# The first block's shift and scale from TensorE in quarters of the channels, and the ahead-of-time weight splits through another pool and VectorE

## The chip, the cores and the metric

The kernel runs on one core of a Trainium2 chip. The metric is the time of one execution of the whole program on the device in microseconds (us), here the median of several runs. TensorE's clock has two levels, 1.2 and 2.4 GHz; the profile gives the share of it that was granted.

## The reference, cut to what matters

Two layers work on 512 tokens of 1024 channels, 256 context tokens and 256 latent tokens. Each layer has a feed-forward block, a mixer of four token mixers, and a second feed-forward block. Every block first normalises its input and then shifts and scales it per channel; shift, scale and gate come from a vector of the stream (context or latent) through one large matrix per layer:

```
mod   = (silu(c)     @ ada_w[l] + ada_b[l]).reshape(1, 1, 3, 3, D)     # latent tokens
mod_c = (silu(c_ctx) @ ada_w[l] + ada_b[l]).reshape(1, 1, 3, 3, D)     # context tokens

def ffn_step(s, m, j, f):
    hm = layer_norm(s) * (1 + m[:, :, j, 1]) + m[:, :, j, 0]           # modulate: scale, shift
    y = swiglu(hm, ffn_w_in[f], ffn_w_out[f])
    return post_norm(s, 0.5 * m[:, :, j, 2] * y, j)                    # m[j, 2]: gate
```

`ada_w[l]` is 1024 x 9216 in 32-bit floats: 9 groups (3 blocks, and shift, scale and gate in each) of 1024 columns. The two groups that the change is about, shift and scale of block 0 of layer 0, are 8 MB of it. `w_in[l]`, the input matrix of the mixer, is cut into 70 chunks of 128 columns.

## The kernel before, in words

All matrix products of the big weights are done with three matmuls in place of one: each operand is split into a rounded high part (ScalarE casts, L123, L159) and the rest as the low part (a subtraction on GpSimd or VectorE, L124, L161), and high x high, high x low and low x high are summed in PSUM (`mm3`, L413 to L415). Weights come as pairs of raw chunks; the list `self.lo` says chunk by chunk whether GpSimd (P) or VectorE (D) subtracts.

`first` (L318) is the start of the program. It loads the tokens, takes the mean and variance on VectorE (L348 to L351), and normalises on ScalarE (L355). Then it goes over the eight channel groups k of 128 channels. For each k it needs shift and scale of 128 channels and two streams: four dot products over 1024 values, each one VectorE instruction (L374) over a transposed 128 x 1024 piece of `ada_w` and a copy of silu(c) on all partitions (`cb`), with a sum at its end. For k above 3 one of the four is a product on GpSimd (L370) and a sum on ScalarE (L371). `cb` is made by a matmul with a column of ones (L340) and Silu on ScalarE (L341). After the dots, two small VectorE instructions add the bias (L381) and 1 (L382); four transposes of the normalised tokens (L385) land in PSUM, ScalarE shifts and scales them in two halves (L390), and `split` (L159, L161) gives the two parts of `H[k]`.

What follows is the first feed-forward block (`ffn`, with `start` set to the two weight pairs that `first` loaded): for each k, 12 matmuls of 512 columns go into four PSUM banks, 96 matmuls in all; I call these the start block. After it come the other weight chunks in order. Between them, at points written in the code (`fill.pop(0)()`), lie fillers: the dot products for all other shifts, scales and gates (`ada_dot`, L199 loads and L203 multiplies), and in two of the four feed-forward blocks `presplit`.

`presplit` (L127) takes one chunk of layer 1's `w_in` in two halves of 512 columns: it loads the half on SyncE's queue (L136), ScalarE casts the high part (L138) and writes it to DRAM (L139, ScalarE's queue), GpSimd subtracts (L140) and writes the low part to DRAM (L141, GpSimd's queue). The mixer of layer 1 then only loads both parts. 38 chunks are done so: 14 in the second feed-forward block of layer 0 and 24 in the first of layer 1, 76 halves in all. Its three tiles come from the pool T (six tiles of 128 x 512). Pool C (two tiles) serves the post-norm at the end of a feed-forward block and the convolution in the mixer.

Other pools: F (five), Y (four) and B (two) hold tiles of 128 x 2048; PSUM has three banks for pm, three for pg and two for px. The instruction order of each engine is not written by hand: a planner goes through the program in order of priority with estimated durations, hands out the tiles, and fixes for every engine and every queue one order. On the chip each queue goes through its order and waits where it has to.

Of the kernel before, what the change touches and what calls it, by code (L numbers as in the profile page):

```python
# [52 lines left out]
class Net:  # L53
# [73 lines left out]
    def presplit(self, l, i):  # L127
        nc = self.nc
        dst = self.dr.tile([P, 2048], F32, name=f"pre{l}_{i}")
        self.pre[l, i] = dst  # L130

        def go():
            for k in range(2):
                c = slice(k * 512, (k + 1) * 512)
                raw = self.T()
                nc.sync.dma_start(raw, self.t["win"][l, i][:, c])  # L136
                h, lo = self.T(F32R), self.T(F32R)
                nc.scalar.copy(h, raw)  # L138
                nc.scalar.dma_start(dst[:, c], h.bitcast(F32))  # L139
                nc.gpsimd.tensor_sub(lo, raw, h.bitcast(F32))  # L140
                nc.gpsimd.dma_start(dst[:, 1024 + k * 512:1024 + (k + 1) * 512], lo.bitcast(F32))  # L141

        return go
# [14 lines left out]
    def split(self, hi, lo, src, pool_lo=True):  # L158
        self.nc.scalar.copy(hi, src)  # L159
        eng = self.nc.gpsimd if pool_lo else self.nc.vector  # L160
        eng.tensor_sub(lo, src, hi.bitcast(F32))  # L161
# [156 lines left out]
    def first(self):  # L318
        nc = self.nc
        V = nc.vector  # L320
        row = self.slot("B", name="row")[:1]
        nc.sync.dma_start(row, self.t["cc"].rearrange("s d -> (s d)").unsqueeze(0))
        ones = self.small(P, "vn")
        V.memset(ones, 1.0)
        self.x = [self.Y(name="x") for _ in range(2)]
        wa = []

        def load_ada():
            k = len(wa)
            wa.append(self.slot("FY"[k % 2], name="wa").rearrange("p (a c) -> p a c", a=2))  # L330
            nc.sync.dma_start(wa[k], self.t["adaw"][0, k:k + KD + 1:KD].rearrange("a p c -> p a c"))

# [3 lines left out]
        load_ada()  # L336
        self.cb = self.sb.tile([P, 2, D], F32, tag="B", bufs=2, name="cb")
        for e in range(4):
            ps = self.ps()
            nc.tensor.matmul(ps, ones[:1], row[:, e * 512:(e + 1) * 512], start=True, stop=True)  # L340
            nc.scalar.activation(self.cb[:, e // 2, (e % 2) * 512:(e % 2 + 1) * 512], ps, AF.Silu)  # L341
        xn = []
        for s in range(2):
# [7 lines left out]
            last = V.scalar_tensor_tensor(nm, mv[:, 0::2], -1.0, r, op0=ALU.mult, op1=ALU.mult)  # L351
# [4 lines left out]
        H = self.new_h()  # L356
        m, ab = self.modT[0], self.adab[:, 0]
        ws = []
        for k in range(KD):
            pair = slice(k, k + KD + 1, KD)  # L360
            if k and k < KD - 1:
                load_ada()
            w = wa[k]
            with self.tc.issue_after(last.ins) if k == 1 else nullcontext():
                for a in range(2):
                    for s in range(2):
                        acc = m[:, k + KD * a, s:s + 1]
# [8 lines left out]
                if k < 2:  # L376
                    self.lo = "P"
                    ws.append(self.pair(self.t["f1"][0, 0, 2 * k:2 * k + 2], "F", (None, "F" if k else None)))
                    if not k:
                        load_ada()  # L380
            V.tensor_add(m[:, pair], m[:, pair], ab[:, pair].unsqueeze(2).to_broadcast([P, 2, 2]))  # L381
            V.tensor_scalar(m[:, k + KD], m[:, k + KD], 1.0, None, op0=ALU.add)  # L382
            ps = self.ps("pg")
            for t in range(4):
                nc.tensor.transpose(ps[:, t * P:(t + 1) * P], xn[t][k // 4][:, k % 4 * P:(k % 4 + 1) * P], self.ident)  # L385
            hf = self.T()
            for s in range(2):
                c = slice(256 * s, 256 * s + 256)
                sh, sc = m[:, k, s:s + 1], m[:, k + KD, s:s + 1]
                nc.scalar.activation(hf[:, c], ps[:, c], AF.Identity, bias=sh, scale=sc)  # L390
            self.split(H[0][:, k], H[1][:, k], hf, pool_lo=k > 2)
# [1148 lines left out]
def lay(a):  # L1540
# [7 lines left out]
    o["adab"] = c(a["ada_b"].reshape(L, 72, P).transpose(2, 0, 1))  # L1548
    o["norm_g"], o["norm_b"] = c(a["norm_g"]), c(a["norm_b"])
# [51 lines left out]
```

## Time and profile before

| | us |
|---|---|
| median of 3 runs | 2805.08 |
| the runs | 2803.21 to 2805.39 |
| profiled execution | 2813.55 |
| its span in the trace | 2811.8 |
| TensorE busy | 2603.6 (93%) |
| VectorE busy | 1937.6 (69%) |
| ScalarE busy | 1101.7 (39%) |
| GpSimd busy | 1017.2 (36%) |

One execution was profiled. PE is TensorE's matmuls, PEld its weight loads, DVE is VectorE, ACT ScalarE, POOL GpSimd, and SP SyncE, which here only issues DMAs. Matmuls are pipelined, and a "busy" TensorE need not be at its full pace; the count of matmuls in a stretch tells more than the busy time.

### The profile page before, as it was taken

What the parts mean: (1) busy time and instruction counts of PE and PEld (TensorE: products, weight loads), DVE (VectorE), ACT (ScalarE), POOL (GpSimd) and SP (SyncE); (2) the same over time, 40 slices, a digit from 0 to 9 for tenths busy, and PEclk for the clock granted to TensorE, in tenths of its full rate; (3) what the DMA queues carried; (4) which work ended last, traced back from release to release, by engine and by line L of the source; (5) the groups of instructions that cost most, each with busy time, mean ns of one, the idle gap of its engine ahead of it and who ended that gap; (6) DMA issues with size and microseconds to landing.
All of it is one profiled execution on the core that took longest, in us unless ns stands there. A gap on an engine that the chain in (4) does not pass through costs nothing.

```text
span 2811.8 us, 38509 instructions
## 1 busy us (share of the span) xinstructions
PE 2603.6 (93%) x14382; PEld 2182.3 (78%) x14382; DVE 1937.6 (69%) x3150; ACT 1101.7 (39%) x2033; POOL 1017.2 (36%) x784
## 2 busy tenths in 40 slices
PE   5999989998898999999989999999999989888998
PEld 3787878776776787879768888777887977777897
DVE  8695966768899835265887662629568899756455
ACT  3322235483333434354322353332444544344443
POOL 4323223222544344436542336662310056411221
PEclk8999999999999999999999999999999999999899
DMA  5555542234432334437874438875364764357353
GB/s 225 188 180 172 191 156 98 73 109 130 137 108 84 113 124 120 164 105 258 293 258 151 164 113 283 309 260 199 103 229 165 237 184 147 124 158 254 120 189 105
DMA packets 195372, 476.73 MB, mean 170 GB/s; under 512 B 32641, under 2 KB 72801, under 8 KB 194161
## 3 DMA queue, kind: packets, MB, share of 16 engines
q1 hardware_dynamic: 174242, 424.40, 46.0%
q10 hardware_dynamic: 14832, 29.89, 3.0%
q0 software_dynamic: 6112, 19.99, 1.9%
q8 instruction: 113, 1.85, 0.3%
q14 instruction: 73, 0.60, 0.1%
HBM read 400.77 MB, written 73.45 MB: 169 GB/s over the span
## 4 chain that ended last, share of the span: by engine, by line
PE 31%; DVE 10%; DMA 6%; issue 4%; POOL 2%; ACT 2%; SPq 0%; ACTq 0%; POOLq 0%; DVEq 0%
PE pm L414 8%; PE pm L415 8%; PE pm L413 8%; DVE junk L203 3%; DMA T<-in_win_dram 2%; DVE wl L124 2%; DMA wa<-in_adaw_dram 1%; DMA pre<-T 1%; DMA wr<-in_wo_dram 1%; DVE G L898 1%; PE px L415 1%; PE px L414 1%; PE px L413 1%; DVE C L1141 1%; PE pg L907 0%
## 5 line engine op out<-in xcount | busy, mean ns | idle before, releaser
L415 PE MATMUL pm<-h,wl 128*128 128x512 f32 (+1 forms) x2512 | 897.7, 358 | 34.9 <-DVE wl L124 34.2
L413 PE MATMUL pm<-h,wh 128*128 128x512 f32 (+1 forms) x2512 | 900.3, 360 | 29.5 <-ACT h L159 12.1
L414 PE MATMUL pm<-h,wh 128*128 128x512 f32 (+1 forms) x2512 | 896.5, 357 | 12.1 <-DVE h L161 6.3
L415 PEld LDWEIGHTS pm<-h,wl 128*128 128x128 f32 x2512 | 488.1, 194 | 109.2 <-DVE wl L124 41.6
L413 PEld LDWEIGHTS pm<-h,wh 128*128 128x128 f32 x2512 | 487.4, 195 | 101.8 <-ACT h L159 14.6
L123 ACT CAST wh<-wr 128x1024 fp32r<-128x1024 f32 x304 | 318.7, 1049 | 605.9 <-PE pm L414 206.6
L414 PEld LDWEIGHTS pm<-h,wh 128*128 128x128 f32 x2512 | 488.7, 195 | 80.8 <-POOL h L161 9.1
L124 DVE TENSOR_TENSOR wl<-wr,wh 128x1024 fp32r<-128x1024 f32 x196 | 276.3, 1410 | 288.8 <-ACT wh L123 287.4
L124 POOL TENSOR_TENSOR wl<-wr,wh 128x1024 fp32r<-128x1024 f32 x108 | 277.6, 2571 | 418.2 <-ACT wh L123 385.3
L203 DVE SCALAR_TENSOR_TENSOR junk<-wa,cb 128x1024 bf16<-128x1024 f32 x256 | 382.1, 1535 | 2.7 <-DMA wa<-in_adaw_dram 1.8
L161 POOL TENSOR_TENSOR F<-G,F 128x512 fp32r<-128x512 f32 (+1 forms) x94 | 135.2, 1439 | 352.3 <-ACT F L159 328.1
L1141 DVE SCALAR_TENSOR_TENSOR C<-C,vec 128x482 f32<-128x482 f32 (+29 forms) x240 | 176.0, 733 | 4.5 <-ACT C L1133 1.4
L414 PE MATMUL pm<-wl,F 128*128 128x512 f32 x368 | 145.6, 396 | 1.7 <-DVE wl L124 1.3
L413 PE MATMUL pm<-wh,F 128*128 128x512 f32 x368 | 145.5, 396 | 1.6 <-ACT G L425 1.6
L415 PE MATMUL pm<-wh,F 128*128 128x512 f32 x368 | 144.1, 395 | 0.0
L140 POOL TENSOR_TENSOR T<-T 128x512 fp32r<-128x512 f32 x76 | 110.6, 1456 | 81.8 <-ACT T L138 80.5
L427 DVE TENSOR_TENSOR G<-G,pm 128x512 f32<-128x512 f32 (+1 forms) x93 | 54.4, 585 | 121.7 <-PE pm L415 97.4
L902 POOL TENSOR_TENSOR wk<-wk,cd 128x512 f32<-128x512 f32 x56 | 70.4, 1259 | 135.6 <-PE pg L924 88.4
L124 DVE TENSOR_TENSOR wl<-raw,wh 128x1024 fp32r<-128x1024 f32 x61 | 75.0, 1231 | 63.5 <-ACT wh L123 63.5
L159 ACT CAST F<-G 128x512 fp32r<-128x512 f32 (+1 forms) x94 | 50.9, 541 | 160.3 <-DVE G L427 160.3
L606 DVE SCALAR_TENSOR_TENSOR G<-pm,vec,G 128x506 f32<-128x506 f32 (+5 forms) x126 | 87.3, 693 | 23.5 <-ACT G L601 21.8
L123 ACT CAST wh<-raw 128x1024 fp32r<-128x1024 f32 x64 | 66.8, 1047 | 85.8 <-PE pm L414 40.7
(411 smaller groups left out, 4595.0 us busy)
## 6 DMA issues: line engine op xcount, KB each, us to landing
wr<-in_f_dram SPq DMA_DIRECT2D x204, 512.0 KB, 4.1
wa<-in_adaw_dram SPq DMA_DIRECT2D x72, 1024.0 KB, 5.1
wr<-in_win_dram SPq DMA_DIRECT2D x94, 512.0 KB, 3.6
raw<-in_f_dram SPq DMA_DIRECT2D x30, 1024.0 KB, 5.0
T<-in_win_dram SPq DMA_DIRECT2D x76, 256.0 KB, 4.9
pre<-T ACTq DMA_DIRECT2D x76, 256.0 KB, 4.1
pre<-T POOLq DMA_DIRECT2D x76, 256.0 KB, 4.5
wl<-pre SPq DMA_DIRECT2D x36, 512.0 KB, 5.2
```

What stands on the lines that cost most here:

```text
L123: nc.scalar.copy(h, r)
L124: (nc.gpsimd if pool_lo else nc.vector).tensor_sub(l, r, h.bitcast(F32))
L140: nc.gpsimd.tensor_sub(lo, raw, h.bitcast(F32))
L161: eng.tensor_sub(lo, src, hi.bitcast(F32))
L203: nc.vector.scalar_tensor_tensor(junk, w3[:, a], 1.0, self.cb[:, s], op0=ALU.mult, op1=ALU.mult, accum_out=self.modT[l][:, i + a, s:s + 1])
L413: nc.tensor.matmul(ps, wh, xh, start=first, stop=False)
L414: nc.tensor.matmul(ps, wh, xl, start=False, stop=False)
L415: nc.tensor.matmul(ps, wl, xh, start=False, stop=last)
L427: nc.vector.tensor_mul(hf[:, c], sg[:, c], pu[:, c])
L606: nc.vector.scalar_tensor_tensor(acc[:, :, d:], src[:, :, :n - d], w(j), acc[:, :, d:], op0=ALU.mult, op1=ALU.add)
L902: nc.gpsimd.tensor_mul(S(d, n + 1).rearrange("p (h e) -> p h e", h=4), S(d, n).rearrange("p (h e) -> p h e", h=4), gs["cd"][:, d * N_CH + ...
L1141: V.scalar_tensor_tensor(o, x, w(j), o, op0=ALU.mult, op1=ALU.add)
```

## The change

There are two parts.

In `presplit` the loaded half comes from pool C in place of T, and the subtraction is done by VectorE in place of GpSimd. The write of the low part stays on GpSimd's queue.

In `first` the dot products go. The two groups of `ada_w` come in their own layout (1024 rows on the partitions, `ada0`), in four quarters q of 256 channels, shift and scale of a quarter in 1 MB each, into tiles of the pools Y, B and F. silu(c) lies as 32 columns per row group, two of them filled (`ct`). For each quarter 16 matmuls with 32 stationary columns and 256 moving columns run in four column groups of the array (partitions 0, 32, 64 and 96 of one PSUM bank), each group summing two of the eight row groups; VectorE copies the bank to SBUF (a tile of T); four matmuls with a two-column selector `sel` add the four groups and turn the result so that channels lie on partitions; VectorE adds the bias and 1. The transposes of the two channel groups of the quarter stand ahead of these matmuls in the program. Shift and scale of the tokens is now half on ScalarE and half on VectorE, and all splits of `H` subtract on VectorE; two of the four splits of the first weights go to VectorE as well (`self.lo = "PD"`). `cb`, which the later dot products need, is loaded and put through Silu by `load_c` (L176) after the last split.

```
 presplit
-                raw = self.T()
+                raw = self.unit("C")
                 nc.sync.dma_start(raw, self.t["win"][l, i][:, c])
                 ...
-                nc.gpsimd.tensor_sub(lo, raw, h.bitcast(F32))
+                nc.vector.tensor_sub(lo, raw, h.bitcast(F32))
 split
-        self.nc.scalar.copy(hi, src)
+        self.last = self.nc.scalar.copy(hi, src).ins
 first
-        row = self.slot("B", name="row")[:1]
-        nc.sync.dma_start(row, self.t["cc"].rearrange("s d -> (s d)").unsqueeze(0))
-        ones = self.small(P, "vn")
-        V.memset(ones, 1.0)
+        cs = self.T()
+        raw, sel = cs[:, 256:272], cs[:, 272:274]
+        nc.scalar.dma_start(cs[:, 256:274], self.t["ccT"])
...
-        load_ada()
-        self.cb = self.sb.tile([P, 2, D], F32, tag="B", bufs=2, name="cb")
-        for e in range(4):
-            ps = self.ps()
-            nc.tensor.matmul(ps, ones[:1], row[:, e * 512:(e + 1) * 512], start=True, stop=True)
-            nc.scalar.activation(self.cb[:, e // 2, (e % 2) * 512:(e % 2 + 1) * 512], ps, AF.Silu)
+        def load_ada(q):
+            for kind in range(2):
+                w = self.slot(("YB", "FF", "YB", "YB")[q][kind], name="wa")
+                nc.sync.dma_start(w, self.t["ada0"][q, kind])
+                wa[q, kind] = w.rearrange("p (k c) -> p k c", k=KD)
+        def load_w(k):
+            self.lo = "PD"
+            ws.append(self.pair(self.t["f1"][0, 0, 2 * k:2 * k + 2], "F", (None, "F" if k else None)))
+        load_ada(0)
+        load_w(0)
+        load_ada(1)
+        V.memset(cs[:, :256], 0.0)
+        ct = cs[:, :256].rearrange("p (k c) -> p k c", k=KD)
+        nc.scalar.activation(ct[:, :, :2], raw.rearrange("p (k s) -> p k s", k=KD), AF.Silu)
...
-        for k in range(KD):
...
-                        if k > 3 and a and s:
-                            j = self.sb.tile([P, D], F32, tag="R", bufs=2, name="prod")
-                            nc.gpsimd.tensor_mul(j, w[:, a], self.cb[:, s])
-                            nc.scalar.activation(j, j, AF.Identity, accum_out=acc)
-                        else:
-                            j = self.sb.tile([P, D], BF16, tag="M", bufs=2, name="junk")
-                            V.scalar_tensor_tensor(j, w[:, a], 1.0, self.cb[:, s], op0=ALU.mult, op1=ALU.mult,
-                                                   accum_out=acc)
...
+        for q in range(4):
+            if q == 1:
+                load_w(1)
+            if q in (1, 2):
+                load_ada(q + 1)
+            pk = []
+            for k in (2 * q, 2 * q + 1):
+                ps = self.ps("pg")
+                for t in range(4):
+                    nc.tensor.transpose(ps[:, t * P:(t + 1) * P], xn[t][k // 4][:, k % 4 * P:(k % 4 + 1) * P],
+                                        self.ident)
+                pk.append(ps)
+            pa = self.ps("pg")
+            for kind in range(2):
+                o = slice(256 * kind, 256 * kind + 256)
+                for r in range(2):
+                    for i in range(4):
+                        nc.tensor.matmul(pa[32 * i:32 * i + 32, o], ct[:, 4 * r + i], wa[q, kind][:, 4 * r + i],
+                                         start=r == 0, stop=r == 1)
+            sb = self.T()
+            nc.vector.tensor_copy(sb, pa)
+            pt = self.ps("px")[:, :8]
+            for i in range(4):
+                nc.tensor.matmul(pt[:, 2 * i:2 * i + 2], sb[:, i * P:(i + 1) * P], sel, start=True, stop=True)
+            k2 = slice(2 * q, 2 * q + 2)
+            V.tensor_add(m4[:, :, k2], pt.rearrange("p (a k s) -> p a k s", a=2, k=2),
+                         ab4[:, :, k2].unsqueeze(3).to_broadcast([P, 2, 2, 2]))
+            V.tensor_scalar(m4[:, 1, k2], m4[:, 1, k2], 1.0, None, op0=ALU.add)
+            for k, ps in zip((2 * q, 2 * q + 1), pk):
+                hf = self.T()
+                for s in range(2):
+                    c = slice(256 * s, 256 * s + 256)
+                    sh, sc = m[:, k, s:s + 1], m[:, k + KD, s:s + 1]
+                    if s:
+                        V.tensor_scalar(hf[:, c], ps[:, c], sc, sh, op0=ALU.mult, op1=ALU.add)
+                    else:
+                        nc.scalar.activation(hf[:, c], ps[:, c], AF.Identity, bias=sh, scale=sc)
+                self.split(H[0][:, k], H[1][:, k], hf, pool_lo=False)
+        with self.tc.issue_after(self.last):
+            self.load_c()
```

## Rows read from the trace of the kernel before

**Rows 1.** Windows of 40 us: length, busy us and count per engine, PEclk, DMA share, GB/s
```profile
40.00:80.00 40.00, 26.02 (x91) 18.44 (x90) 39.67 (x57) 14.14 (x26) 20.11 (x9) 0.81 0.43 151
...
1400.00:1440.00 40.00, 32.83 (x124) 26.05 (x125) 40.00 (x48) 12.11 (x17) 22.75 (x14) 0.87 0.86 295
1440.00:1480.00 40.00, 35.51 (x148) 28.41 (x148) 26.03 (x30) 11.81 (x15) 14.22 (x10) 0.96 0.64 220
...
1720.00:1760.00 40.00, 40.00 (x176) 32.71 (x175) 17.56 (x15) 14.84 (x20) 27.54 (x26) 1.00 0.86 282
```
**Rows 2.** Groups of VectorE's instructions in the first 84 us, busy us and mean ns
```profile
L374 DVE SCALAR_TENSOR_TENSOR junk<-wa,cb 128x1024 bf16<-128x1024 f32 x28 | 47.1, 1716 | 0.0
```
**Rows 3.** Waits in the first 90 us: total us, times, longest
```profile
ACT T L390 <- DVE modT L382: 32.3, 6, 12.0
```
**Rows 4.** Timeline of TensorE at the start block: start us, us, instruction, idle before
```profile
66.14 0.63 PE L414 MATMUL pm<-h,wh 128*128 128x512 f32 x1
66.57 0.63 PE L415 MATMUL pm<-h,wl 128*128 128x512 f32 x1
...
81.57 0.39 PE L415 MATMUL px<-h,wF 128*128 128x512 f32 x1
...
86.50 0.80 PE L415 MATMUL pm<-h,wl 128*128 128x512 f32 x1 [2.36 <-DVE wl L124]
```
**Rows 5.** Windows of 5 us at the start, columns as in the first group
```profile
0.00:5.00 5.00, 2.13 (x3) 1.12 (x4) 0.22 (x2) 1.34 (x2) 0.93 (x5) 1.00 0.52 170
...
10.00:15.00 5.00, 0.05 (x2) 0.03 (x1) 4.39 (x13) 1.49 (x3) 1.18 (x2) 1.00 1.03 418
```
**Rows 6.** Timeline of ScalarE: the normalised tokens
```profile
14.11 5.75 ACT L355 ACTIVATE G<-x,bnm,br 128x512 f32<-128x512 f32 x8 [3.45 <-DVE bnm L351]
```
**Rows 7.** Timeline of TensorE in layer 0's mixer, small fp32 matmuls (two records each)
```profile
768.03 1.35 PE L1275 MATMUL px<-ident,T 128*128 128x128 f32 x8
769.31 0.64 PE L888 MATMUL pg<-wk,gt 128*32 128x128 f32 x16
769.88 1.10 PE L1281 MATMUL px<-kv,T 128*128 128x64 f32 x8
...
772.83 1.95 PE L907 MATMUL pg<-vn,G 128*128 128x128 f32 x16
```
**Rows 8.** Groups of VectorE's instructions over the whole span
```profile
L911 DVE TENSOR_TENSOR wk<-pg,wk 128x512 f32<-128x512 f32 x56 | 38.2, 684 | 11.3 <-PE pg L907 10.9
...
L427 DVE TENSOR_TENSOR G<-G,pm 128x256 f32<-128x256 f32 x34 | 14.3, 421 | 50.3 <-PE pm L415 40.5 <-POOL F L161 4.0 <-ACT G L425 3.6
```
**Rows 9.** Groups of ScalarE's instructions in the first 84 us
```profile
L390 ACT ACTIVATE T<-pg,modT 128x256 f32<-128x256 f32 x16 | 8.1, 559 | 32.3 <-DVE modT L382 32.3
...
L159 ACT CAST h<-T 128x512 fp32r<-128x512 f32 x8 | 5.0, 619 | 0.3
```
**Rows 10.** Tile cb at its second load, 1200 to 1320 us: ns min/median/max
```profile
L182 ACT ACTIVATE cb<-cb x2: 1062/1062/1062, 1226.6 to 1228.0; 128x1024 f32<-128x1024 f32 x2
...
DMA to landing us min/median/max: 6.4/6.9/7.4
```
**Rows 11.** Timeline of VectorE: first and last step of the first gate, its first use
```profile
71.60 1.21 DVE L203 SCALAR_TENSOR_TENSOR junk<-wa,cb 128x1024 bf16<-128x1024 f32 x1
...
102.90 2.36 DVE L210 TENSOR_TENSOR modT<-modT,adab 128x16 f32<-128x16 f32 x1
...
144.30 1.28 DVE L560 TENSOR_TENSOR M<-pm,gate 128x512 f32<-128x512 f32 x2
```
**Rows 12.** Tile T: subtraction of the presplits; idle of engines before instructions on T
```profile
L140 POOL TENSOR_TENSOR T<-T x76: 1257/1296/2272, 1281.4 to 1886.4; 128x512 fp32r<-128x512 f32 x76
...
  ACT T L138: 81.0, 41
```
**Rows 13.** Timelines of VectorE and GpSimd at one presplit
```profile
1404.25 2.28 DVE L203 SCALAR_TENSOR_TENSOR junk<-wa,cb 128x1024 bf16<-128x1024 f32 x1
...
1403.19 2.27 POOL L140 TENSOR_TENSOR T<-T 128x512 fp32r<-128x512 f32 x1 [4.90 <-ACT T L138]
```

More of the change, by code (lines that the diff above doesn't have):

```diff
@@ L320, in first @@
         V = nc.vector
-        row = self.slot("B", name="row")[:1]
-        nc.sync.dma_start(row, self.t["cc"].rearrange("s d -> (s d)").unsqueeze(0))
-        ones = self.small(P, "vn")
-        V.memset(ones, 1.0)
+        cs = self.T()
+        raw, sel = cs[:, 256:272], cs[:, 272:274]
+        nc.scalar.dma_start(cs[:, 256:274], self.t["ccT"])
         self.x = [self.Y(name="x") for _ in range(2)]
[L326 to L331, printed above, removed]
         for t in range(4):
@@ L335, in first @@
             nc.sync.dma_start(self.x[t // 2][:, o], self.t["xall"][t // 2][:, o])
-        load_ada()
-        self.cb = self.sb.tile([P, 2, D], F32, tag="B", bufs=2, name="cb")
-        for e in range(4):
-            ps = self.ps()
-            nc.tensor.matmul(ps, ones[:1], row[:, e * 512:(e + 1) * 512], start=True, stop=True)
-            nc.scalar.activation(self.cb[:, e // 2, (e % 2) * 512:(e % 2 + 1) * 512], ps, AF.Silu)
+        wa = {}
+        def load_ada(q):
[3 more added lines that the diff above has]
+                wa[q, kind] = w.rearrange("p (k c) -> p k c", k=KD)
+        ws = []
+        def load_w(k):
[7 more added lines that the diff above has]
+        nc.scalar.activation(ct[:, :, :2], raw.rearrange("p (k s) -> p k s", k=KD), AF.Silu)
         xn = []
@@ L350, in first @@
             r, nm = self.rstd(mv[:, 1::2], LN_EPS, 2, "b"), self.small(2, "bnm", 2)
-            last = V.scalar_tensor_tensor(nm, mv[:, 0::2], -1.0, r, op0=ALU.mult, op1=ALU.mult)
+            V.scalar_tensor_tensor(nm, mv[:, 0::2], -1.0, r, op0=ALU.mult, op1=ALU.mult)
             for e in range(2):
@@ L357, in first @@
         m, ab = self.modT[0], self.adab[:, 0]
-        ws = []
-        for k in range(KD):
[L360 to L367, printed above, removed]
-                        if k > 3 and a and s:
-                            j = self.sb.tile([P, D], F32, tag="R", bufs=2, name="prod")
-                            nc.gpsimd.tensor_mul(j, w[:, a], self.cb[:, s])
-                            nc.scalar.activation(j, j, AF.Identity, accum_out=acc)
-                        else:
-                            j = self.sb.tile([P, D], BF16, tag="M", bufs=2, name="junk")
-                            V.scalar_tensor_tensor(j, w[:, a], 1.0, self.cb[:, s], op0=ALU.mult, op1=ALU.mult,
-                                                   accum_out=acc)
[L376 to L391, printed above, removed]
@@ new lines, in first @@
+        m4 = m[:, :2 * KD].rearrange("p (a k) s -> p a k s", a=2)
+        ab4 = ab[:, :2 * KD].rearrange("p (a k) -> p a k", a=2)
+        for q in range(4):
[36 more added lines that the diff above has]
+                self.split(H[0][:, k], H[1][:, k], hf, pool_lo=False)
@@ L1548, in lay @@
     o["adab"] = c(a["ada_b"].reshape(L, 72, P).transpose(2, 0, 1))
+    w = a["ada_w"][0, :, :2 * D].reshape(KD, P, 2, 4, 256)
+    o["ada0"] = c(w.transpose(3, 2, 1, 0, 4).reshape(4, 2, P, 2048))
+    q = np.arange(P)[:, None] % 32 == np.arange(2)[None, :]
+    o["ccT"] = c(np.concatenate([o["cc"].reshape(2, KD, P).transpose(2, 1, 0).reshape(P, 16), q], 1).astype(np.float32))
     o["norm_g"], o["norm_b"] = c(a["norm_g"]), c(a["norm_b"])
```

## Prediction

> **What bounds the kernel now.** I read the windows first, then the waits and timelines of the two places that the change touches. In a good stretch TensorE does 176 matmuls in 40 us, 0.227 us each, the last row of [rows 1]. Against that pace two places stand out.
>
> The first is the start. In 40 to 80 us TensorE does 91 matmuls while VectorE is busy 39.67 of 40 us [rows 1]. What fills VectorE are the 28 dots of shift and scale, 47.1 us [rows 2]; ScalarE's shift and scale waits 32.3 us for their result [rows 3] and TensorE waits behind it. The last matmul of the start block starts at 81.57 us [rows 4]. So the start is bound by VectorE, and a shorter way to shift and scale moves the whole rest of the program.
>
> The second are the stretches with presplits. In 1400 to 1480 us TensorE does 124 + 148 = 272 matmuls in place of 352, so 80 x 0.227 = 18 us are lost, with VectorE full in the first half [rows 1]. In the other presplit stretch, in layer 1, VectorE is busy 17.56 of 40 us and TensorE loses nothing (the last of [rows 1]).
>
> **Part one, the start.** Three floors for the end of the start block:
>
> - DMA. 2 MB of tokens, 2 MB of weights and 8 MB of `ada_w` are 12.6 million bytes, at 418 GB/s 30 us; the first 5 us run at 170 GB/s, which costs 3 more [rows 5]. All is there at about 33 us. The last quarter waits for tiles of the first, whose matmuls are through by some 25 us, before its turn in the queue, so that costs nothing.
> - TensorE. Per quarter: 8 transposes 1.35 us [rows 7]; 32 records of 256 columns in column groups: 16 records of 128 columns take 0.64 us, of which the last one's own 0.27 (an estimate, from (1.95 - 0.27)/15 = 0.11 per untiled record), so 0.025 each, against 0.11 without column groups; at 256 columns 0.05, 32 x 0.05 + 0.3 = 1.9 us; four selector matmuls are 8 records with a full weight load, 1.10 us [rows 7]; 24 matmuls of the start block 24 x 0.227 = 5.5 us [rows 1]. Sum 9.9 us, four quarters 39 us. It can start when the tokens are normalised, 14.11 + 5.75 = 19.9 us [rows 6], or a few us before with the first quarter. All of it at 2.4 GHz and without a wait: 56 to 59 us. At 1.2 GHz matmuls are 0.43 us apart (66.57 - 66.14 [rows 4]) at 66 us, in a stretch of 40 us with a mean granted clock of 0.81 (the first of [rows 1]).
> - The chain of one quarter: matmuls 1.9, copy from PSUM 0.7 [rows 8], selector 1.1, two small VectorE steps 0.4 (estimate, a fifth of the longer ones), shift and scale of two groups 2 x 0.56 [rows 9], the second half on VectorE beside it at about 0.42 [rows 8], split 0.62 + 0.68 [rows 8, 9]: 6.5 us. The three banks of pg hold two groups of transposes and one of products, so the next quarter starts only when this one is shifted and scaled; but TensorE fills that time with the 5.5 us of the quarter before. VectorE's whole work is eight statistics, four copies, 16 halves and splits, some 20 us by these rows: not the bound.
>
> TensorE's floor is the highest. I add one quarter's chain that nothing fills at the first quarter's end and some 1.2 GHz at first (8 matmuls x 0.2 = 2 us) and take 63 us in place of 82: -19 us. Bounds: -26 (56 us: the first quarter's products done ahead of the tokens, all warm) and -8 (74 us: half of TensorE's 39 us at 1.2 GHz, or chain and matmuls one after the other, 20 + 4 x (6.5 + 5.5) + 6 = 74).
>
> One rule of the Trainium skill speaks against the column groups. The trace first: after 16 column-tiled records at 769.31, the next full-array matmul starts at 769.88, before these end at 769.95, and the eight records take 1.10 us [rows 7]; a change of shape costs nothing to be seen. The page "TensorEngine Tiling (Array Packing)", section "Tiling Modes", says that changing the mode drains the array. If each of some 16 changes (four per quarter, an estimate from the order in the code) cost one record's 0.27 us, part one would be 4 us less. The measured rows decide, and I count nothing.
>
> What is late next at the end of the block: TensorE stands 2.36 us for VectorE's first weight split, up to 86.50 [rows 4]; there dots are queued ahead on VectorE. They now start later, so -1 us, between -2.4 and 0.
>
> What the change adds at the end: `load_c` comes after the last split, on ScalarE's queue: 6.9 us to land and 2 x 1.06 us of Silu [rows 10], so the later dots start at about 57 + 9 = 66 us in place of 71.60 [rows 11]. Measured from the end of the start block that is 13 us later than now. The cover: the first gate's dots end at 102.9 and the gate is first used at 144.3 [rows 11], 41 us of slack. If Silu stands ahead of weight casts in ScalarE's order, these wait up to 7 us. I take +1, bounds 0 and +6.
>
> **Part two, the presplits.** 76 subtractions leave GpSimd (1.30 us in the middle [rows 12]) and come to VectorE at about 0.68 us, by the nearest row of that size, 0.684 [rows 8]; 28 in layer 0's second feed-forward block, 48 in layer 1's first. But GpSimd's subtraction holds up VectorE: a dot that takes 1.21 us alone [rows 11] takes 2.28 us beside one [rows 13], 1.07 us more. So where VectorE is full, moving one gains 1.07 - 0.68 = 0.39 us, and where it idles the 0.68 us is free. In the block of layer 0 I take half of the 28 to collide: 14 x 0.39 = 5.5 us less on VectorE where it sets the pace; about half reaches TensorE: -3. In layer 1 zero.
>
> Against it: the moved instruction waits for ScalarE's cast, which waits for a load. Before instructions on these tiles engines sat 81 us for that cast, 41 times [rows 12]. On VectorE the dots and the weight splits stand behind it, and for those TensorE waits. Also ScalarE's cast now waits for a T tile whose write must have landed, and SyncE's queue waits for a C tile, that is for VectorE, with weight loads behind it; in exchange three halves are under way on T in place of two, and the load no longer waits for a write. The writes keep their queues. Bounds of part two: -10 (half of the 18 us that TensorE loses comes back) and +30 (below).
>
> **Sum**, against the profiled execution of 2813.55 us: -19 - 1 + 1 - 3 = -22 us, 2791.6. The profiled execution is 8.5 us above the median of 2805.08; I let that difference stand and take 2805 - 22 = 2783 us.
>
> **The rivals.**
>
> 1. TensorE becomes the bound of the start and stays cold: products, selector and start block fall into short pieces with waits between, at 0.43 us a matmul, or each quarter's chain runs alone. For: the chain of banks in pg; today's block runs at a granted clock of 0.81 (the first of [rows 1]). Against: the gaps of now are VectorE's dots, which go. The block ends at 74: -8 - 3 = -11, so 2794. Chance 0.17.
> 2. Slower: VectorE's queue stands behind late loads in the presplits. Place: 1300 to 1460 us and the dots late in layer 1's block. Price: the 81 us [rows 12] and 76 x 0.68 = 52 us of new work are 133 us; if 4 in 10 of the presplits fall where VectorE is full (an estimate, from half in layer 0 and a third in layer 1), 53 us, less 30 collisions saved at 1.07 us, leaves 21 us; as much as 9 more for weight loads behind a waiting SyncE makes 30 us. With -19 of part one and its small terms that is +11, 2816. It decides once more than 19 us of it reach TensorE. Against: what VectorE does behind it (weight splits) needs ScalarE, which waits for the same load today. Chance 0.10.
> 3. The stretch of 1400 to 1480 us comes loose: -10 in place of -3, so 2775, and with part one's best 2768. Chance 0.10.
> 4. The gain is given back: dots that begin 13 us later against TensorE leave VectorE full longer in the first block, TensorE waits for weight splits there, 15 to 20 us: no change, 2800 to 2805. Against: the 41 us of slack. Chance 0.08.
>
> **How the numbers follow.** My forecast has 0.55, with its own range 2776 to 2792. A difference under 0.2% (5.6 us) counts as no change. Faster: the forecast, rival 3, 0.16 of rival 1 and 0.02 of the others, 0.83. No change: 0.09, nearly all rival 4. Slower: 0.08, rival 2 and a little of 4. The range of 2767 to 2803 holds rivals 1 and 3 and half of 4.
>
> **What would show it.** No dots before some 60 us; column-tiled records 0.05 us apart; the start block's last matmul near 63 us; the first later dot near 66. In the presplit stretches VectorE's dots back near 1.2 us, SyncE's waits for C short, 1400 to 1480 us above 272 matmuls. The forecast is wrong if the block ends after 74 us, if VectorE shows waits for the presplits' casts with TensorE waiting for weight splits right behind them, or if the span shrinks by less than the start did.

## The result and the profile after

| | median us | runs, range | profiled execution: time, span |
|---|---|---|---|
| before | 2805.23 | 4, 2803.21 to 2807.02 | 2813.55, 2811.8 |
| changed | 2766.82 | 4, 2763.92 to 2767.80 | 2767.44, 2765.7 |

The medians lie 38.4 us apart; the ratio is 0.9856 with a 95% interval of 0.9838 to 0.9873, which is 40 us of 2805. The forecast was 22 us faster, 2783 us, with 2767 as the lower end of its range; the time fell 0.2 us below that end. The direction was right, the size was not. Run again beside other kernels, the changed one gave 0.9859 [0.9834, 0.9885].

The first thing to look at is the start. Windows of 40 us of the changed kernel, columns as in [rows 1]:

```profile
0.00:40.00 40.00, 21.60 (x160) 12.76 (x161) 17.44 (x36) 15.68 (x22) 7.11 (x9) 0.91 0.95 373
40.00:80.00 40.00, 37.78 (x196) 29.29 (x195) 25.16 (x38) 13.06 (x19) 6.96 (x3) 1.00 0.45 147
```

From 40 to 80 us TensorE does 196 matmuls where it did 91, the granted clock is 1.00 (2.4 GHz) where its mean was 0.81, and VectorE is busy 25.16 us where it was full [rows 1]. The timeline of TensorE in the changed kernel says where the block ends (start us, us, instruction, idle before it in brackets):

```profile
12.80 0.69 PE L375 MATMUL pg<-ident,G 128*128 128x128 f32 x2 [12.80 <-ACT G L361]
...
36.20 0.66 PE L375 MATMUL pg<-ident,G 128*128 128x128 f32 x4 [0.27 <-DVE T L400]
36.79 1.93 PE L383 MATMUL pg<-wa,T 128*32 128x256 f32 x32
38.65 0.96 PE L427 MATMUL pm<-h,wh 128*128 128x512 f32 x3
...
42.95 0.95 PE L389 MATMUL px<-T 128*128 128x2 f32 x8
...
62.76 0.39 PE L429 MATMUL px<-h,wF 128*128 128x512 f32 x1
...
64.89 0.50 PE L427 MATMUL pm<-h,wh 128*128 128x512 f32 x1 [0.71 <-ACT G L439]
...
65.58 0.50 PE L429 MATMUL pm<-h,wl 128*128 128x512 f32 x1
```

The start block's last matmul starts at 62.76 us, before at 81.57 [rows 4]. The weight split that TensorE stood 2.36 us for, up to 86.50 [rows 4], is ready here: the same step, a matmul with the low part `wl`, starts at 65.58 without a wait, 20.9 us earlier; what TensorE waits for just before it is ScalarE (0.71 us at 64.89). The dots that come later are not late. Timelines of VectorE and ScalarE in the changed kernel, one fence for each:

```profile
60.80 1.23 DVE L203 SCALAR_TENSOR_TENSOR junk<-wa,cb 128x1024 bf16<-128x1024 f32 x1 [3.87 <-ACT cb L182]
...
124.87 1.28 DVE L574 TENSOR_TENSOR M<-pm,gate 128x512 f32<-128x512 f32 x2
```
```profile
55.50 0.33 ACTq L180 DMA_DIRECT2D cb<-in_cc_dram  x1
...
59.70 1.06 ACT L182 ACTIVATE cb<-cb 128x1024 f32<-128x1024 f32 x1 [3.58 <-DMA cb<-in_cc_dram]
```

The first dot starts at 60.80, before the block has ended, and the gate's first use at 124.87 came forward by 19.4 us against [rows 11], about as far as the end of the start block (18.8 us).

The second place is the presplits. Windows of the changed kernel in both feed-forward blocks that carry them:

```profile
1400.00:1440.00 40.00, 39.65 (x171) 31.66 (x170) 28.48 (x37) 11.03 (x14) 11.92 (x6) 1.00 0.60 207
1440.00:1480.00 40.00, 40.00 (x179) 32.99 (x178) 26.29 (x34) 8.58 (x9) 13.21 (x7) 1.00 0.44 150
...
1760.00:1800.00 40.00, 39.74 (x171) 31.75 (x170) 21.17 (x23) 15.83 (x23) 15.41 (x15) 1.00 0.90 316
1800.00:1840.00 40.00, 38.76 (x168) 31.00 (x167) 13.57 (x15) 15.03 (x20) 14.84 (x12) 1.00 0.68 224
1840.00:1880.00 40.00, 40.00 (x177) 32.78 (x176) 36.67 (x51) 8.14 (x9) 12.74 (x7) 1.00 0.52 170
```

1400 to 1480 us now holds 171 + 179 = 350 matmuls against 272 [rows 1]. The work at a given time is not the same in the two kernels (the changed one is 33 to 42 us ahead there), so stages compare better than windows. From one profiled execution of each, bounded by the writes of `xspill` that end the first block of each layer and the loads of `norm_g` that open the two blocks after layer 0's mixer (before 459.03, 1265.08, 1660.76 and 2054.47 us; changed 433.73, 1231.82, 1618.76 and 2008.32):

| stage, us | before | before again | changed | changed again |
|---|---|---|---|---|
| layer 0 up to its last `xspill` (start, first block) | 459.0 | 455.2 | 433.7 | 435.8 |
| layer 0's mixer | 806.1 | 800.9 | 798.1 | 800.6 |
| layer 0's second feed-forward block (28 presplits) | 395.7 | 398.2 | 386.9 | 384.2 |
| layer 1's first feed-forward block (48 presplits) | 393.7 | 392.9 | 389.6 | 388.6 |
| the rest | 757.3 | 758.0 | 757.3 | 758.7 |
| TensorE's listed waits in the two blocks | 17.3 + 11.2 | 20.0 + 14.3 | 10.2 + 8.0 | 7.5 + 7.1 |

The first profile of before lies 8.3 us above the median, and most of that is in its first stage and its mixer, of which the second is touched by neither part. Against the second one the change is worth -21.5 in the first stage, -2.8 in the mixer, -11.3 and -3.3 in the two blocks and -0.6 in the rest: -39.4 between the spans, up to rounding. So part one gave about what was forecast (-19), and the surplus is in the blocks with presplits, where -3 was forecast.

What fills VectorE in layer 0's second block, groups of its instructions (busy us, mean ns of one, idle before and its releaser). Before, 1265 to 1525 us, with GpSimd's subtraction:

```profile
L203 DVE SCALAR_TENSOR_TENSOR junk<-wa,cb 128x1024 bf16<-128x1024 f32 x69 | 115.7, 1719 | 2.1 <-DMA wa<-in_adaw_dram 1.8
L140 POOL TENSOR_TENSOR T<-T 128x512 fp32r<-128x512 f32 x28 | 47.1, 1684 | 31.0 <-ACT T L138 30.9
L124 DVE TENSOR_TENSOR wl<-wr,wh 128x1024 fp32r<-128x1024 f32 x26 | 35.7, 1372 | 41.5 <-ACT wh L123 41.4
```

The same groups in the changed kernel, 1232 to 1479 us:

```profile
L203 DVE SCALAR_TENSOR_TENSOR junk<-wa,cb 128x1024 bf16<-128x1024 f32 x68 | 99.4, 1498 | 4.7 <-DMA wa<-in_adaw_dram 4.1 <-POOL x L580 0.6
L140 DVE TENSOR_TENSOR T<-C,T 128x512 fp32r<-128x512 f32 x28 | 22.4, 801 | 20.8 <-ACT T L138 18.4 <-DMA pre<-T 2.3
L124 DVE TENSOR_TENSOR wl<-wr,wh 128x1024 fp32r<-128x1024 f32 x26 | 35.8, 1376 | 24.6 <-ACT wh L123 24.6
```

A dot is 0.22 us shorter, 16 us over the group; the subtractions bring 22.4 us to VectorE and 20.8 us of waiting, nearly all for ScalarE's cast. But the wait ahead of the weight splits fell from 41.5 to 24.6 us. Both instructions wait for the same ScalarE, so most of the new wait can stand where VectorE stood anyway; the sums fit that and do not prove it. What reached TensorE is its wait for VectorE's weight splits in this block (us in total, times, longest), before and changed:

```profile
PE pm L415 <- DVE wl L124: 9.6, 4, 4.0
```
```profile
PE pm L429 <- DVE wl L124: 4.2, 4, 1.8
```

### The profile page after: what moved, and what is told of

The parts are those of the page before. It is cut to its first block, busy times and chain, and to the rows that moved or that the text cites. A ratio compares the mean times of both kernels' runs of the same rounds, so it can differ in the third digit from the quotient of the medians.

```text
span 2765.7 us, 38791 instructions
## 1 busy us (share of the span) xinstructions
PE 2597.6 (94%) x14534; PEld 2169.8 (78%) x14534; DVE 1920.4 (69%) x3181; ACT 1094.4 (40%) x2016; POOL 883.3 (32%) x697
## 4 chain that ended last, share of the span: by engine, by line
PE 32%; DVE 9%; DMA 8%; issue 3%; ACT 3%; POOL 1%; SPq 0%; ACTq 0%; DVEq 0%; POOLq 0%
PE pm L429 9%; PE pm L428 9%; PE pm L427 9%; DMA C<-in_win_dram 4%; DVE junk L203 2%; DVE wl L124 1%; DVE T L140 1%; DMA wr<-in_f_dram 1%; DMA wr<-in_wo_dram 1%; PE pg L921 1%; DMA wa<-in_adaw_dram 1%; PE px L429 1%; PE px L428 1%; PE px L427 1%; DVE G L912 1%
## 5 line engine op out<-in xcount | busy, mean ns | idle before, releaser
L429 PE MATMUL pm<-h,wl 128*128 128x512 f32 (+1 forms) x2512 | 896.4, 357 | 19.4 <-DVE wl L124 18.7
L427 PEld LDWEIGHTS pm<-h,wh 128*128 128x128 f32 x2512 | 481.4, 192 | 103.9 <-ACT h L159 12.1
L429 PEld LDWEIGHTS pm<-h,wl 128*128 128x128 f32 x2512 | 481.6, 192 | 98.4 <-DVE wl L124 25.0
L428 PEld LDWEIGHTS pm<-h,wh 128*128 128x128 f32 x2512 | 482.0, 192 | 78.7 <-POOL h L161 8.0
L203 DVE SCALAR_TENSOR_TENSOR junk<-wa,cb 128x1024 bf16<-128x1024 f32 x256 | 366.3, 1471 | 10.8 <-DMA wa<-in_adaw_dram 5.7
L140 DVE TENSOR_TENSOR T<-C,T 128x512 fp32r<-128x512 f32 x76 | 67.1, 883 | 85.7 <-ACT T L138 83.2
L124 DVE TENSOR_TENSOR wl<-raw,wh 128x1024 fp32r<-128x1024 f32 x62 | 76.3, 1232 | 61.6 <-ACT wh L123 61.6
L123 ACT CAST wh<-raw 128x1024 fp32r<-128x1024 f32 x64 | 67.1, 1051 | 86.8 <-PE pm L428 40.2
```

The costliest lines, as they stand in the source:

```text
L123: nc.scalar.copy(h, r)
L124: (nc.gpsimd if pool_lo else nc.vector).tensor_sub(l, r, h.bitcast(F32))
L140: nc.vector.tensor_sub(lo, raw, h.bitcast(F32))
L203: nc.vector.scalar_tensor_tensor(junk, w3[:, a], 1.0, self.cb[:, s], op0=ALU.mult, op1=ALU.mult, accum_out=self.modT[l][:, i + a, s:s + 1])
L427: nc.tensor.matmul(ps, wh, xh, start=first, stop=False)
L428: nc.tensor.matmul(ps, wh, xl, start=False, stop=False)
```

## Experiments

Three readings of the surplus stood against each other. Pool C: before, SyncE's next load waited for a write from a T tile to land, and with C this wait goes. Contention: GpSimd's subtraction lengthens VectorE's instructions more than was counted. And the planner: other tiles and other engines change the written order, and that by itself is worth this much. Each ratio is to the kernel before, run beside it. The median of the kernel before differed between these groups of runs (2805.23, 2806.75, 2808.47 and 2812.02 us), so a difference in microseconds is taken from the ratios, times 2805, and not from the medians.

**Part one alone**: the changed kernel with the two lines of `presplit` as before.

```
-                raw = self.unit("C")
+                raw = self.T()
-                nc.vector.tensor_sub(lo, raw, h.bitcast(F32))
+                nc.gpsimd.tensor_sub(lo, raw, h.bitcast(F32))
```

> Part one alone: the new start with TensorE, presplits as before (pool T, GpSimd subtracts). Kernel before 2805, with both parts 2767. Theory A (the start is worth its 19 to 21 us at the end of the start block and some 4 us more in the first feed-forward block, where fewer weight splits are late; the presplits are worth the rest): 2780, that is -25, span of the first feed-forward block to its end 25 us earlier, the stretch of layer 0's second feed-forward block as long as before. Theory B (the start is worth 20 us and nothing later; the rest is all the presplits'): 2785, first feed-forward block's end 20 us earlier. Theory C (the other order that the planner comes to is worth 8 us in layer 0's mixer, which neither part touches): 2772.

Measured: 2788.27 us, 0.9928 [0.991, 0.9947], -20 us. Its first stage is 434.4 us long, as in the changed kernel; its blocks 395.9 and 395.3, as before. Part one did what was forecast, and at its place.

**Part two alone**: the kernel before with the same two lines changed.

> Part two alone: presplits load into pool C and subtract on VectorE, the start as before. Theory A: -13, 2792, nine of it in layer 0's second feed-forward block and four in layer 1's first. Theory B: -18, 2787. Theory C (the mixer's 8 us come with the new start's order): -10, 2795. The start as in the kernel before, last matmul of the start block at 81 to 82 us, in all three. My forecast had -3, 2802.

Measured: 2781.32 us, 0.9897 [0.9878, 0.9915], -29 us; first stage 456.2, blocks 383.0 and 383.9. The listed waits of TensorE in the blocks are 10.4 and 6.1 us. The forecast had -3 for this part and -10 as its best bound: this is the step that failed. The two parts don't quite add up: -20 and -29 are -49, and together they gave -40. Each of the three has an interval of some 5 us to either side, so the 9 us are at the edge of what these runs can tell. Layer 1's block is 5 us shorter here (383.9, against 389.6 and 388.6 with both parts), which is no more than single executions differ by.

**Pool C alone**, and **VectorE's subtraction alone**: the kernel before with one of the two lines each.

> Only the pool of the presplits' load changed to C; GpSimd still subtracts; start as before. Theory P (what helps is that a load on SyncE's queue no longer waits for a T tile whose write to DRAM must land, 26.5 us of SyncE's waits in layer 0's second feed-forward block): -8 to -10, 2796, these waits gone. Theory G (what helps is GpSimd's subtraction gone, which holds VectorE up by 1.07 us each): no change, 2805, VectorE's later dots still 2.28 us beside a subtraction.

> Only the subtraction of the presplits moved to VectorE; loads still into pool T; start as before. Theory P: no change or a little slower, 2803 to 2812, SyncE's waits for landed writes as before. Theory G: -8 to -10, 2796, mean of the dots in layer 0's second feed-forward block shorter. If both are needed, e3 and e4 both show less than half of what the two together give.

Measured: C alone 2799.1 us, 0.9953 [0.9935, 0.9971], -13; the subtraction alone 2792.6 us, 0.9948 [0.9929, 0.9968], -15. Together that is -28, where both at once gave -29. So the pool, to which the forecast gave no number, is nearly half of part two by these ratios. The two blocks take 391.5 and 390.9 us with C alone, 389.2 and 386.2 with the subtraction alone; against before (395.7 and 398.2, 393.7 and 392.9) the first pair is little more than the spread of single executions. With pool C alone VectorE's dots in layer 0's block (1259 to 1513 us) are as long as before:

```profile
L203 DVE SCALAR_TENSOR_TENSOR junk<-wa,cb 128x1024 bf16<-128x1024 f32 x68 | 112.8, 1699 | 1.2 <-DMA wa<-in_adaw_dram 0.6 <-POOL x L566 0.5
```

and with VectorE's subtraction alone (1256 to 1509 us) they are short:

```profile
L203 DVE SCALAR_TENSOR_TENSOR junk<-wa,cb 128x1024 bf16<-128x1024 f32 x68 | 101.0, 1517 | 0.8 <-POOL x L566 0.5 <-DMA wa<-in_adaw_dram 0.3
```

The short dots come from the engine, not from the pool. TensorE's waits for VectorE's weight splits in layer 0's block go with them: 11.0 us with C alone, as before (10.9 and 12.7), and 4.4 with the subtraction alone, as in the changed kernel (4.2 and 3.1). What the pool takes away is a wait of SyncE's queue. Its waits (us in total, times, longest), before, in the two blocks (1265 to 1660, 1661 to 2055 us):

```profile
SPq L136 <- DMA pre<-T: 26.5, 10, 4.4
...
SPq L136 <- DMA pre<-T: 49.6, 14, 5.5
```

With pool C alone, in layer 0's block (1259 to 1513 us):

```profile
SPq L136 <- POOL T L140: 42.2, 17, 12.8
```

The load no longer waits for a write but for the subtraction that frees its C tile. And two halves are loaded ahead: the first two loads start at 952 and 957 us, in the mixer, where before the first comes at 1277 us. The sum of SyncE's waits is hardly less (342 us against 341 to 346 over layer 0's block): the queue runs as far ahead as tiles allow and always waits for something. By which path the 13 us reach TensorE stays open: its own listed waits are 16.0 + 14.3 us with C alone, inside what before shows twice.

**No subtraction at all**: the start as before, pool C, and the high part written in place of the low part, so that the low parts of layer 1's weights are left out.

```
-                h, lo = self.T(F32R), self.T(F32R)
+                h = self.T(F32R)
...
-                nc.vector.tensor_sub(lo, raw, h.bitcast(F32))
-                nc.gpsimd.dma_start(dst[:, 1024 + k * 512:1024 + (k + 1) * 512], lo.bitcast(F32))
+                nc.gpsimd.dma_start(dst[:, 1024 + k * 512:1024 + (k + 1) * 512], h.bitcast(F32))
```

> The start as before, presplits with the load in pool C and no subtraction at all: the high part is written twice (the low parts of layer 1's input weights are left out). Against the same with GpSimd's subtraction (0.9953 of the kernel before) and with VectorE's (0.9897). Theory G: VectorE's subtraction is nearly free where VectorE idles and GpSimd's costs its collisions, so 0.987 to 0.990, at most 8 us below VectorE's. Theory V (VectorE's 52 us of new work cost much and are only less bad than GpSimd's): 0.980 to 0.984, 15 to 25 us below.

Measured: 2780.14 us, 0.9911 [0.989, 0.9931]; blocks 379.4 and 386.6. This gives the price of the subtraction on either engine. On VectorE (0.9897) it cannot be told from none. On GpSimd (0.9953) it costs 0.0042 of 2805 us, 12 us, and the intervals just fail to meet. TensorE's listed waits say the same: 8.4 + 7.4 us here, 10.4 + 6.1 with VectorE, 16.0 + 14.3 with GpSimd. So the subtraction has a price on GpSimd and none that shows on VectorE. Without `lo` one T tile per half is free as well; since VectorE's version holds that tile and loses nothing by it, it is not the price.

That GpSimd lengthens the dots can be read off the traces dot by dot. In none of the fourteen profiles here did a dot take more than 1.23 us when GpSimd ran nothing beside it. Of the 96 dots in layer 0's block, 29 to 31 took more than 1.3 us where GpSimd subtracts, 16 to 18 where VectorE does or nobody, as long as GpSimd keeps its weight splits. How much of the 12 us comes this way is not shown: GpSimd's slower subtraction (1.68 us on average in that block, VectorE's 0.80) also holds its tiles longer, and no run changed the one without the other.

**The same load put back on GpSimd**: the changed kernel, and GpSimd does two subtractions of 256 columns on the cast half, whose result nobody reads.

```
+                d = self.sb.tile([P, V_N], F32, tag="vec", bufs=1, name="dum")
+                for e in range(2):
+                    nc.gpsimd.tensor_sub(d[:, :256], h[:, 256 * e:256 * e + 256].bitcast(F32),
+                                         h[:, 256 * e:256 * e + 256].bitcast(F32))
```

> The changed kernel (2767), and beside each presplit subtraction on VectorE GpSimd subtracts the cast half from itself in two pieces of 256 columns into a tile that nothing reads, in place of the work that it lost (the extra instructions compute nothing that is used). The load's tile is still set free by VectorE. Theory G (what the move of the subtraction gave is that GpSimd no longer holds VectorE up beside the dots): +10 to +15, 2780, dots in layer 0's second feed-forward block back from 1.50 to 1.70 us. Theory L (what it gave is a shorter way from load to free tile, and so an earlier next load): 2767 to 2770, though the dots are longer again.

Measured: 2798.16 us, 0.9966 [0.9952, 0.9981], some 30 us slower than the changed kernel; the blocks take 401.3 and 402.2 us. Groups of layer 0's block (1232 to 1495 us; its lines stand four lower):

```profile
L207 DVE SCALAR_TENSOR_TENSOR junk<-wa,cb 128x1024 bf16<-128x1024 f32 x69 | 105.4, 1560 | 5.0 <-DMA wa<-in_adaw_dram 4.3 <-POOL x L584 0.6
...
L140 DVE TENSOR_TENSOR T<-C,T 128x512 fp32r<-128x512 f32 x28 | 27.0, 972 | 12.1 <-DMA pre<-T 7.0 <-ACT T L138 5.1
```

The dots and the subtractions are longer, by 6.0 and 4.6 us in sum. That is not the 14 to 17 us by which the block grew: GpSimd also holds the T tile of the cast half longer and issues the write of the low part behind its own work. So this run shows that elementwise work on GpSimd costs time here although nobody reads its result. TensorE's wait for VectorE's weight splits in layer 0's block is back at 10.0 us. But the run does not show that contention is all of it.

**The load into pool G**: the changed kernel with `raw = self.G()`.

> The changed kernel with the presplits' load in pool G (eight tiles, of which the hidden activations use up to four) in place of C (two). Theory P2 (SyncE's queue still waits for a free load tile, 38 + 11 us in layer 0's second feed-forward block of the changed kernel, and weight loads behind it are late): -4 to -8, 2761, these waits near zero. Theory E (two tiles are enough: what a queue waits there it would wait at the next load): within 3 us of the changed kernel, since the loads already take 0.8 to 0.9 of the DMA engines' time.

Measured: 2783.63 us, 0.9919 [0.9897, 0.994], 17 us slower than the changed kernel run beside it. It was meant to tell whether the number of tiles counts, and does not. The loads of the halves in the changed kernel (number, ns min/median/max, first and last start):

```profile
L136 SPq DMA_DIRECT2D C<-in_win_dram x76: 327/328/1007, 923.6 to 1811.0; - x76
```

and with G:

```profile
L136 SPq DMA_DIRECT2D G<-in_win_dram x76: 327/424/1472, 1414.4 to 1955.9; - x76
```

With G the first load starts only at 1414 us, 180 us into layer 0's block, so the presplits run late, mostly in layer 1's block; the blocks take 393.5 and 396.0 us. SyncE waits for these loads only 3 us in each block, and the kernel is slower all the same. A short wait of a queue is no sign that the order is good. This fits the planner's reading, in which the choice of a pool moves the whole stretch; which instructions lose by it was not traced.

**No column groups**: each quarter's products run one row group after the other on 32 columns of the array; the copy and the selector take 32 partitions.

```
-                for r in range(2):
-                    for i in range(4):
-                        nc.tensor.matmul(pa[32 * i:32 * i + 32, o], ct[:, 4 * r + i], wa[q, kind][:, 4 * r + i],
-                                         start=r == 0, stop=r == 1)
+                for i in range(KD):
+                    nc.tensor.matmul(pa[:32, o], ct[:, i], wa[q, kind][:, i], start=i == 0, stop=i == KD - 1)
```

> The changed kernel, with the 16 matmuls of a quarter all in one column group (8 row groups summed in partitions 0 to 31, the selector matmuls over 32 partitions). A record of 256 columns then takes 0.21 us in place of 0.05, 32 records 6.8 in place of 1.9 us, +5 us a quarter. Theory T (TensorE sets the pace of the start block): +15 to +20, 2785, start block's end at about 80. Theory D (the loads or the chain of a quarter set it and TensorE has slack): +0 to +5, 2770.

Measured: 2786.74 us, 0.9931 [0.9908, 0.9955], 20 to 21 us slower than the changed kernel. Timeline of TensorE:

```profile
31.00 7.09 PE L382 MATMUL pg<-wa,T 128*32 128x256 f32 x32
...
84.20 0.39 PE L427 MATMUL px<-h,wF 128*128 128x512 f32 x1
```

32 records take 7.09 us in place of 1.93, and the block ends at 84.20, 2.6 us later than it ended before the change. The gain of part one hangs on the four column groups: 4 x 5.16 = 20.6 us of TensorE time, nearly the whole difference.

**Both kernels again**, unchanged, for the spread.

> The changed kernel again, beside the next three: 0.985 to 0.987 of the kernel before. Layer 0's second feed-forward block (first norm row load to the next one) within 4 us of the 387 us of its first profile.

> The kernel before, unchanged, for a second profile: how far apart two profiles of one kernel lie stage by stage. The first profile was 8.5 us above the median, and layer 0's mixer took 806 us in it against 798 to 802 in the profiles of five kernels that do the same there. If that is the spread of executions, this one has about 800 there; if it is the order that the planner gave, again 806.

Measured: 2767.1 us, 0.9859 [0.9834, 0.9885], and 2806.89 us in one run. Their stages stand in the table above: stages that are the same program differ by up to 5 us between single executions (800.9 and 806.1). So the 806.1 of the first profile is the spread of executions, and a difference of that size in one stage of one profile is not a finding.

**GpSimd's other subtractions**: if its elementwise work costs that much, more of it should go. First the feed-forward's weight splits, all to VectorE:

```
-        self.lo = "D" if lat else "DDP"
+        self.lo = "D"
```

> The changed kernel, and in all feed-forward blocks VectorE does all weight splits (in three of the four blocks GpSimd did one of three). A GpSimd split takes 2.6 us and holds VectorE up by 2.2, a VectorE split takes 1.14. Theory G: where dots fill VectorE each of the moved splits frees 1 us of it, and about half of that reaches TensorE: -5 to -10, 2760. Theory W (VectorE's own work decides, collisions are rare): +5 to +15, 2777, VectorE fuller in these blocks.

Measured: 2761.14 us, 0.9831 [0.9809, 0.9853], by the ratios 7 us below the changed kernel, with intervals that overlap. The first stage is 13 us shorter (420.6), the mixer 9 us longer (809.5). Then the splits of the hidden rows too:

```
-        self.split(hid[i // 4][0][:, oc], hid[i // 4][1][:, oc], hf[:, c])
+        self.split(hid[i // 4][0][:, oc], hid[i // 4][1][:, oc], hf[:, c], pool_lo=False)
```

> All weight splits of the feed-forward blocks on VectorE (as in the run before that moved them, -7), and the splits of the hidden activations too (GpSimd 1.3 to 1.5 us each, VectorE 0.68). Theory G: another -3 to -8 beyond that run, 2754, dots near 1.23 us. Theory F (VectorE is full without them by now, and a split that waits for ScalarE's cast holds up the dots): 0 to +6 against that run, 2764.

Measured: 2754.39 us, 0.9813 [0.9788, 0.9837], 52 us under before and 13 us under the changed kernel run beside it (2767.1, 0.9834 to 0.9885). It beats both kernels; the two intervals touch, but its slowest run, 2757.95, is below the fastest of the changed kernel, 2762.20. Of the 96 dots in layer 0's block one took more than 1.3 us; their mean is 1.23. Its mixer, which neither edit touches directly, takes 809.6 us, 9 us more than in the others; that both runs show it makes it more than the spread, but its cause is open.

## Why the prediction was wrong, step by step

**The bound at the start** was right. VectorE's dots set it; without them TensorE has work without long waits, at a granted clock of 0.91 up to 40 us and 1.00 after, and the block ends at 62.76 us against a forecast of 63. That it came so near is partly luck: TensorE began at 12.80 us, where the sum begins at 19.9 or a few us before, and took 50 us from there, not 43. The terms: 32 records in column groups 1.93 us (forecast 1.9, worked out from the 0.64 us of [rows 7]), the selector's eight records 0.95 (1.10), the copy 0.69 (0.7). Part one alone measured -20 against the -19, -1 and +1 of the sum.

**Rival 1**, a cold start at 2794 us, did not come: the block did not end at 74 us, and from 40 to 80 us TensorE did 196 matmuls at a granted clock of 1.00.

**The change of shape** was counted at nothing, and the trace gives no sign of the 4 us: the column-tiled records at 36.79 start before the transposes in front of them end (36.20 + 0.66 = 36.86), and the next full-array matmul starts at 38.65, before they end at 38.72. The end of the block is no proof either way, since other terms of the sum were off by more.

**`load_c` and the late dots**: +1 forecast, nothing found. The first dot came at 60.80 in place of 66 us: the load, issued at 55.50, had landed by 59.70, 4.2 us where 6.9 was taken, and the dot began after the first of the two Silus. Rival 4 fell with it.

**The presplits** are the step that failed: "about half reaches TensorE: -3. In layer 1 zero", and of the pool "in exchange three halves are under way on T in place of two, and the load no longer waits for a write", with no number to it. The part is worth -29 alone and some -20 on top of part one (40 - 20). Three errors went into it.

- Pool C was named and not priced. Alone it is -13 us. A row that called for a term was at hand, SyncE's 26.5 and 49.6 us of waiting for writes from T, though it would not have given the size: those waits went, others took their place, and how the gain reaches TensorE is still open.
- The subtraction was sized by a sum of busy times: 1.07 us saved on a dot against 0.68 us added, for half of 28. Of the 96 dots in layer 0's block some 14 fewer are lengthened, as many as the sum took. But the subtraction took 0.80 us, and 16 us saved stand against 22.4 added by all 28, of which the sum charged 14 at 0.68. And yet TensorE waits less: the likely reason, argued from the sums and not shown, is that the added instructions stand in VectorE's waits for ScalarE and the lengthened dots did not. None at all (0.9911) is no faster than 76 on VectorE (0.9897).
- That in layer 1 "TensorE loses nothing" came from one window, 1720 to 1760 us, with 176 matmuls. The next three of the same block, before:

```profile
1760.00:1800.00 40.00, 38.33 (x167) 30.89 (x165) 35.10 (x36) 13.42 (x18) 24.63 (x21) 1.00 0.88 301
1800.00:1840.00 40.00, 38.28 (x162) 31.50 (x163) 12.33 (x12) 16.31 (x23) 25.98 (x23) 0.96 0.91 307
1840.00:1880.00 40.00, 38.36 (x166) 30.74 (x165) 8.00 (x7) 16.48 (x23) 27.96 (x27) 1.00 0.85 281
```

They lack 9, 14 and 10 matmuls, 33 x 0.227 = 7.5 us. With these three windows the bound of part two would have been some -18 rather than -10, and the low end of the range below what came.

**Rival 2**, VectorE's queue behind late loads, was wrong in its price. The waits for the casts are there (18.4 us in layer 0's block), but they take the place of waits for weight casts. Those of TensorE for VectorE's weight splits, which it had growing, fell.

**Rival 3** (2768 us) was the nearest in time, and that is partly luck (its own terms give 2776 and, with part one's best, 2769). Its mechanism, the stretch in layer 0 coming loose, is the larger part of what happened, 11.3 of the 14.6 us in the two blocks; but it reached 2768 only with 26 us from part one, which gave 20, and it has no term for the pool or for layer 1.

**The signs.** Two that the forecast named for the presplits did not come, though the time fell further than it said: the dots are at 1.50 us on average, not near 1.2, and SyncE's waits for the subtractions that free C tiles are not short, 37.6 us in layer 0's block.

## What to carry to other kernels

Give each tile that changes its pool a term of its own, as for an instruction, and run it alone: the queue's list of waits shows what the load waits for, but not what that is worth. Read every window of a stretch, not one. What moved work costs on its new engine is not its busy time: VectorE is busy 67.1 us with the 76 subtractions, and the kernel shows no cost of them, probably since that engine was waiting there anyway. Leaving the work out altogether is a cheap run that gives its price. And when a kernel is bound by TensorE with VectorE close behind, as here, try to take elementwise work off GpSimd even though it looks idle.

## What the runs showed of the hardware that was not expected

GpSimd's elementwise work is not free beside a busy VectorE. Where its 28 subtractions ran in layer 0's block, VectorE's dots took 1.70 to 1.74 us on average; where VectorE did them itself, 1.49 to 1.52, and 1.51 without any. The Trainium skill, "SBUF — State Buffer", section "Who interferes with whom", says that a VectorE instruction with both inputs in SBUF and a GpSimd instruction that reads SBUF exclude each other, and that the later one waits for the whole of the other. The trace agrees in kind: a dot of 1.21 us alone took 2.28 beside a subtraction of 2.27 [rows 11, 13]. What the runs add is the price in a whole kernel, 12 us for 76 subtractions (0.9953 against 0.9911).

Four column groups are worth nearly their number, 3.7 times: the same 32 records of 256 columns in fp32 took 1.93 us in four groups and 7.09 us in one, both at a granted clock of 1.00 (from 28 to 40 us in the run without groups; the changed kernel from 40 us on, where a quarter again took 1.93).
